# The first norm's row through DRAM instead of through TensorE

## The chip, the cores and the metric

The kernel runs on one core of one Trainium2 chip. The metric is the device time of one execution in microseconds; the median over the runs is compared. The engines are named as in the profile: PE (TensorE products) and PEld (its weight loads), DVE (VectorE), ACT (ScalarE), POOL (GpSimd), SP (SyncE, which issues nearly all transfers of this kernel).

## The reference, cut to what matters

One decoder layer on 1024 tokens of width 1024: RMSNorm, one input projection for two mixers (a gated delta rule with four heads of 128, and a dilated window attention with eight heads of 64), an output projection with residual, a second RMSNorm, a gated MLP with a short convolution, residual, and a last RMSNorm. The change touches the first norm alone:

```python
def rmsnorm(x, w):
    xf = x.astype(jnp.float32)
    y = xf * lax.rsqrt(jnp.mean(xf * xf, axis=-1, keepdims=True) + EPS)
    return (y * w.astype(jnp.float32)).astype(x.dtype)
...
    h = rmsnorm(x, norm1_w)
    proj = h @ w_in
```

The factor `rsqrt(mean(x^2) + EPS)` is one number per token. The kernel pulls it behind the projection: it multiplies x by the norm's weights only, projects, and multiplies the projection's columns by the token's factor when they leave PSUM.

## The kernel before

Activations lie transposed, with channels on the 128 partitions and the 1024 tokens along the row. Every float32 matrix is split into a high part (xhi, whi) and a rest (xlo, wlo), and a product is three products of such parts (`mm3`, L203). One product writes 512 tokens into one PSUM bank, so that a block of 128 output channels is two banks of 24 products (eight channel blocks of x by three).

The program is written as coroutines (`first`, `norms`, `gates`, `dense`, `kprep` and others), which a planner, `Weave`, runs in turn. The planner keeps a clock of PE by written estimates; a coroutine yields how long it would still wait, and the most urgent one that is ready goes on. The order that comes out is fixed for PE (`tp` and `mm` stamp an issue order on each instruction, L191 and L195). The order on the other engines and on the transfer queue is set by the framework's scheduler, which places an instruction where its inputs are ready in a simulated timeline, with the program's order as priority.

What the steps touch:

- While x is loaded, DVE adds up the squares of its eight channel blocks into `acc` (L281 on). `first` (L356) runs the first 144 products: three key blocks, into six banks `pst`, which are the two slots of each of the rings hf, asc and ch.
- `norms` (L370) sums `acc` over the partitions with eight small products, one per 128 tokens, so that the sums of the 1024 tokens lie as 128 x 8. DVE scales them (`rst`, L367), and POOL takes them to the power -1/2 (`rsqrt`, L238). Then the row has to lie on every partition, since it multiplies along the tokens: for each half, four transposes of a column of `rst`, repeated 128 times, fill a bank of the ring atr, and DVE copies it into `rstdB` (L368, 128 x 1024).
- `gates` (L396) runs beside it. It needs `rst`, not `rstdB`. At its end the running sums of the decay go to DRAM (`gdram<-grow`), and `kprep` (L577) reads them back on every partition, once for each of four heads (`dec<-gdram`).
- `scaled` (L444) multiplies a pair of banks by `rstdB`, half by half, and so empties them: `xr<-ps,rstdB` for keys, queries, values and gates, `aqkv<-ps,rstdB` for the attention. `first_keys` (L498) does it for the six banks of `first`, and goes on with the convolution of the keys on ACT and DVE (`kT`).
- `dense` (L505) waits for `first` and `norms` in the planner, loads the next weight blocks (`wst<-in_wi`), and runs the other 25 column blocks, each in two banks of the ring hf, which has two slots. A bank is overwritten only when `scaled` has emptied it.

`sy` is the wrapper around the SP queue (L139 is the wrapper's line, so all DVE, ACT, POOL and SP instructions recorded through it have that line). `rstdB` is used again, with other contents, in the second and the last norm; those are not touched.

Of the kernel before, what the change touches and what calls it, by code (L numbers as in the profile page):

```python
# [7 lines left out]
F32 = mybir.dt.float32  # L8
# [7 lines left out]
P = 128  # L16
# [128 lines left out]
def hybrid_layer(tc, I, out):  # L145
    nc = tc.nc
    wv = Weave()
    ve = Engine(wv, nc.vector, "vector", 0.07, 0.00105)
# [5 lines left out]
    sy = Engine(wv, nc.sync, "sync", 0.05, 0.00142, 2.2)  # L154
# [8 lines left out]
    dp = es.enter_context(tc.tile_pool(name="dp", bufs=1, space=DRAM))  # L163
# [15 lines left out]
    def const(name, shape, src=None):  # L179
        t = cp.tile(list(shape), F32, name=name)  # L180
        if src is not None:
            sy.dma_start(t, src)
        return t
# [6 lines left out]
    def mm(dst, lhs, rhs, us, start=True, stop=True, **kw):  # L190
        tc.stamp_issue_order_token(nc.tensor.matmul(dst, lhs, rhs, start=start, stop=stop, **kw).ins, TOKEN)  # L191
        wv.product(us, dst, lhs, rhs)

    def tp(dst, src):
        tc.stamp_issue_order_token(nc.tensor.transpose(dst, src, ident).ins, TOKEN)  # L195
        wv.product(0.11, dst, src)
# [41 lines left out]
    def rsqrt(dst, src, n):  # L238
        po_.tensor_tensor(dst, src, mhalf[:, :n], op=OP.pow)


    mixer = dp.tile([8, P, S], F32, name="mixer")
    mdram = dp.tile([H, 32, 1024], F32, name="mdram")
    gdram = dp.tile([NCH * H, P], F32, name="gdram")
# [8 lines left out]
    def bank(tag, name="ps"):  # L253
        return tile_(pp_, (P, 512), F32, name, tag, 2)

    def next_bank(tag, *tiles, slack=0.0):

        while max(wv.need(*tiles), wv.slot_free(tag, 2)) + slack > 1e-3:
            yield max(wv.need(*tiles), wv.slot_free(tag, 2)) + slack
        return bank(tag)  # L260

    def half(i):
        return slice(i * 512, i * 512 + 512)
# [103 lines left out]
    rst = const("rst", [P, NCH])  # L367
    rstdB = const("rstdB", [P, S])  # L368

    def norms():  # L370
        yield wv.need(acc, slack=8.0)
        ssp = yield from next_bank("atr", acc)
        for c in range(NCH):
            mm(ssp[:, c:c + 1], acc[:, c * P:(c + 1) * P], ones[:, :1], 0.215)
            if c % 2:
                yield APART
        ve.tensor_scalar(rst, ssp[:, :NCH], 1.0 / 1024, EPS, op0=OP.mult, op1=OP.add)
        rsqrt(rst, rst, NCH)
        wv.done.add("rst")
        yield wv.need(rst)  # L380
        for h in range(2):
            if h:
                yield wv.need(rstdB, slack=0.3)
            pb = yield from next_bank("atr")
            for c in range(4):
                i = 4 * h + c
                tp(pb[:, c * P:(c + 1) * P], rst[:, i:i + 1].to_broadcast([P, P]))
            ve.tensor_copy(rstdB[:, half(h)], pb)
        wv.done.add("norms")

    beta = sp.tile([P, NCH, H], F32, name="beta")
# [1242 lines left out]
    def mlp_down():  # L1634
# [56 lines left out]
        final_norm(0, right, ("hf", "ch"), more=squares)  # L1691

    wv.add(0, norms())
    wv.add(1, gates())
    wv.add(9, first())
# [71 lines left out]
```

## Time and profile before

| what | value |
| --- | --- |
| runs, median of 3 | 1205.56 us (1205.49 to 1207.72) |
| profiled execution, span | 1204.1 us |
| PE busy | 1194.7 us, 99% |
| DVE busy | 957.1 us, 79% |
| ACT busy | 575.9 us, 48% |
| POOL busy | 54.3 us, 5% |
| granted TensorE clock, mean | 0.998 |

The profile is of one execution, and its span runs from the first to the last instruction; the device time of a run holds some more around it. A row of a group has the source line, the engine, the operation, the tiles it writes and reads with their shapes, the count, the busy time and the mean of one. A row of the timeline has the start and the length in us, and in brackets how long the engine had been idle before and what released it. A row of the chain of waits has the start, the length and the engine whose work the end of the program hung on. A row of transfers has the queue, the count, the size of one and the median time from issue to landing. Matmuls are pipelined, so that their recorded lengths overlap; the distance from start to start is the pace.

### The profile page before, as it was taken

What the parts mean: (1) busy time and instruction counts of PE and PEld (TensorE: products, weight loads), DVE (VectorE), ACT (ScalarE), POOL (GpSimd) and SP (SyncE); (2) the same over time, 40 slices, a digit from 0 to 9 for tenths busy, and PEclk for the clock granted to TensorE, in tenths of its full rate; (3) what the DMA queues carried; (4) which work ended last, traced back from release to release, by engine and by line L of the source; (5) the groups of instructions that cost most, each with busy time, mean ns of one, the idle gap of its engine ahead of it and who ended that gap; (6) DMA issues with size and microseconds to landing.
All of it is one profiled execution on the core that took longest, in us unless ns stands there. A gap on an engine that the chain in (4) does not pass through costs nothing.

```text
span 1204.1 us, 18360 instructions
## 1 busy us (share of the span) xinstructions
PE 1194.7 (99%) x7058; PEld 987.9 (82%) x7058; DVE 957.1 (79%) x1530; ACT 575.9 (48%) x1131; POOL 54.3 (5%) x50
## 2 busy tenths in 40 slices
PE   9999999999999999999999999999999999999997
PEld 7888887898777777888888888888888888888887
DVE  7686985474667687767898989889898889898987
ACT  7383344364444444555554544444454454445452
POOL 0212110023000000000000000000000000000001
PEclk9999999999999999999999999999999999999999
DMA  7323234426433323443123132231322296357734
GB/s 236 106 75 102 77 119 122 157 79 212 166 115 106 106 63 123 150 140 140 56 85 106 59 100 89 69 105 53 105 71 86 94 370 227 109 179 223 242 97 157
DMA packets 81704, 152.72 MB, mean 127 GB/s; under 512 B 21552, under 2 KB 32592, under 8 KB 81616
## 3 DMA queue, kind: packets, MB, share of 16 engines
q1 hardware_dynamic: 80896, 151.02, 38.3%
q8 instruction: 55, 0.90, 0.3%
q10 hardware_dynamic: 720, 0.53, 0.1%
q14 instruction: 33, 0.27, 0.1%
HBM read 113.49 MB, written 35.93 MB: 124 GB/s over the span
## 4 chain that ended last, share of the span: by engine, by line
PE 98%; DVE 1%; ACT 0%; issue 0%; POOL 0%; DVEq 0%; ACTq 0%; POOLq 0%
PE ps L191 48%; PE pa L191 20%; PE dw L191 17%; PE pc L191 10%; PE ps L195 2%; PE ps L200 1%; PE warm L191 0%; DVE x1h L139 0%; ACT sm L141 0%; PE pd L191 0%; DVE sm L141 0%; POOL rs L139 0%; DVE xr L139 0%; ACT u L139 0%; ACT sq L139 0%
## 5 line engine op out<-in xcount | busy, mean ns | idle before, releaser
L191 PE MATMUL dw<-pr 128*128 128x512 f32 (+1 forms) x984 | 211.4, 377 | 0.0
L191 PEld LDWEIGHTS dw<-pr 128*128 128x128 f32 x984 | 176.8, 188 | 33.5
L191 PE MATMUL ps<-xhi,whi 128*128 128x512 f32 x448 | 186.4, 416 | 0.0
L191 PE MATMUL ps<-xhi,wlo 128*128 128x512 f32 x448 | 175.8, 392 | 0.0
L191 PE MATMUL ps<-xlo,whi 128*128 128x512 f32 x448 | 175.4, 391 | 0.0
L191 PE MATMUL pa<-T,pair 128*128 128x512 f32 x528 | 127.1, 390 | 0.1
L191 PEld LDWEIGHTS pa<-T,pair 128*128 128x128 f32 x528 | 99.0, 188 | 20.9 <-ACT u L139 0.5
L191 PEld LDWEIGHTS ps<-xhi,whi 128*128 128x128 f32 x448 | 84.7, 189 | 19.4 <-issue 2.7
L191 PEld LDWEIGHTS ps<-xhi,wlo 128*128 128x128 f32 x448 | 84.3, 188 | 18.4
L191 PEld LDWEIGHTS ps<-xlo,whi 128*128 128x128 f32 x448 | 84.9, 189 | 13.7
L139 ACT ACTIVATE u<-pa 128x512 f32<-128x512 f32 x44 | 26.3, 599 | 109.7 <-PE pa L191 109.7
L139 DVE SCALAR_TENSOR_TENSOR y<-xu,fcw,y 128x1023 f32<-128x1023 f32 (+1 forms) x44 | 56.4, 1281 | 24.4 <-ACT y L139 24.4
L139 ACT ACTIVATE pr<-wd 128x1024 fp32r<-128x1024 f32 x33 | 35.0, 1061 | 73.9 <-DVE wd L139 36.9
L139 ACT ACTIVATE whi<-wst 128x1024 fp32r<-128x1024 f32 (+2 forms) x38 | 38.6, 1015 | 62.7 <-PE ps L191 55.7
L191 PE MATMUL pa<-B,A 128*128 128x512 f32 x264 | 63.5, 390 | 0.0
L191 PE MATMUL pa<-T,S 128*128 128x512 f32 x264 | 63.4, 390 | 0.0
L191 PE MATMUL pc<-T,S 128*128 128x512 f32 x264 | 63.4, 390 | 0.0
L191 PE MATMUL pc<-B,pair 128*128 128x512 f32 x264 | 63.4, 390 | 0.0
L139 DVE TENSOR_TENSOR wst<-wst 128x512 f32<-128x512 f32 x88 | 60.5, 687 | 0.8
L191 PE MATMUL ps<-B,pair 128*128 128x512 f32 x252 | 60.6, 390 | 0.0
L141 ACT ACTIVATE sm<-sm,mx 128x128 f32<-128x128 f32 (+7 forms) x64 | 35.5, 555 | 48.1 <-DVE mx L141 48.1
L191 PEld LDWEIGHTS pa<-T,S 128*128 128x128 f32 x264 | 49.6, 188 | 10.2
(240 smaller groups left out, 2253.1 us busy)
## 6 DMA issues: line engine op xcount, KB each, us to landing
wst<-in_wu SPq DMA_DIRECT2D x44, 512.0 KB, 3.7
wd<-in_wd SPq DMA_DIRECT2D x44, 512.0 KB, 4.5
wst<-in_wi SPq DMA_DIRECT2D x25, 512.0 KB, 3.7
upark<-y SPq DMA_DIRECT2D x22, 512.0 KB, 3.7
r<-upark SPq DMA_DIRECT2D x22, 512.0 KB, 10.2
apark<-aqkv SPq DMA_DIRECT2D x12, 512.0 KB, 3.0
wa<-in_wd SPq DMA_DIRECT2D x22, 256.0 KB, 3.0
wst<-in_wo SPq DMA_DIRECT2D x8, 512.0 KB, 3.8
```

Of the source, the lines that this page charges most:

```text
L139: return getattr(eng, op)(*a, **kw)
L141: return getattr(eng, op)(*a, **kw)
L191: tc.stamp_issue_order_token(nc.tensor.matmul(dst, lhs, rhs, start=start, stop=stop, **kw).ins, TOKEN)
L195: tc.stamp_issue_order_token(nc.tensor.transpose(dst, src, ident).ins, TOKEN)
L200: tc.stamp_issue_order_token(nc.tensor.transpose(dst, src[rows], ident[rows, rows]).ins, TOKEN)
```

## The change

After `rsqrt`, the two rounds of four transposes and a copy go. In their place a new helper, `spread`, writes the 128 x 8 numbers of `rst` to a row of 1024 in DRAM in the order of the tokens, and reads this row back onto all 128 partitions of `rstdB`. Both transfers are issued on SP's queue; the second waits for the first through the DRAM tile. `norms` no longer yields after `rst`, so that the planner takes it as done at once. The row is a DRAM tile of 8 x 128 float32.

```diff
+    def spread(dst, src, name):
+
+        n_ = src.shape[-1]
+        row = dp.tile([n_, P], F32, name=name)
+        sy.dma_start(row.rearrange("c p -> p c"), src)
+        sy.dma_start(dst, bass.AP(tensor=row.tensor, offset=row.offset, ap=[[0, P], [1, n_ * P]]))
...
         wv.done.add("rst")
-        yield wv.need(rst)
-        for h in range(2):
-            if h:
-                yield wv.need(rstdB, slack=0.3)
-            pb = yield from next_bank("atr")
-            for c in range(4):
-                i = 4 * h + c
-                tp(pb[:, c * P:(c + 1) * P], rst[:, i:i + 1].to_broadcast([P, P]))
-            ve.tensor_copy(rstdB[:, half(h)], pb)
+        spread(rstdB, rst, "rrow")
         wv.done.add("norms")
```

## The prediction

> **What bounds the kernel now.** I read the page first, for the engine that is never idle, then the chain of waits around the norm, then the timelines of the engines that the row passes through.
>
> ```profile
> span 1204.1 us, 18360 instructions
> PE 1194.7 (99%) x7058; PEld 987.9 (82%) x7058; DVE 957.1 (79%) x1530; ACT 575.9 (48%) x1131; POOL 54.3 (5%) x50
> PE 98%; DVE 1%; ACT 0%; issue 0%; POOL 0%; DVEq 0%; ACTq 0%; POOLq 0%
> ```
>
> ```profile
> 5.74 31.71 PE ps L191 x166
> 37.45 0.44 PE ps L195 x4
> 37.89 2.09 PE ps L191 x9
> 39.98 0.44 PE ps L195 x4
> 40.42 20.47 PE ps L191 x91
> ```
>
> TensorE is the bound from the first products to the tail: 98% of the chain that ended last is PE, and in the norm's stretch one PE piece follows on the other with no gap. The eight transposes of the change are the two L195 pieces, 0.44 us each. They stand on the chain, so what they take is paid in full. The span is 1204.1 us and the median of the runs 1205.56 us, so some 1.5 us lie around the span; I apply the sum to the median.
>
> The row's way through the other engines:
>
> ```profile
> L139 POOL TENSOR_TENSOR rst<-rst,mhalf x1: 1639/1639/1639, 34.0 to 34.0; 128x8 f32<-128x8 f32 x1
> ```
>
> ```profile
> 38.52 0.68 DVE L139 COPY rstdB<-ps 128x512 f32<-128x512 f32 x1
> 40.45 0.69 DVE L139 COPY rstdB<-ps 128x512 f32<-128x512 f32 x1 [1.25 <-PE ps L195]
> ...
> 45.28 3.41 DVE L139 TENSOR_TENSOR xr<-ps,rstdB 128x512 f32<-128x512 f32 x5 [2.32 <-PE ps L191]
> 48.61 1.44 DVE L139 SCALAR_TENSOR_TENSOR kT<-xr,gcw,kT 128x1023 f32<-128x1023 f32 x1
> 49.97 0.68 DVE L139 TENSOR_TENSOR xr<-ps,rstdB 128x512 f32<-128x512 f32 x1
> 50.58 7.29 DVE L139 SCALAR_TENSOR_TENSOR kT<-xr,gcw,kT 128x1023 f32<-128x1023 f32 x4
> 57.79 0.68 DVE L139 TENSOR_TENSOR xr<-ps,rstdB 128x512 f32<-128x512 f32 x1
> ```
>
> rst is ready at 33.96 + 1.64 = 35.60 us, rstdB is whole at 41.14 us, and its first reader starts at 45.28 us, released not by rstdB but by PE, which has only then finished the first bank of keys. So the row is 4.1 us early, and that is the room the change has before anything waits.
>
> **What is removed.** Eight transposes: 2 x 0.44 = 0.88 us of PE on the chain. Two DVE copies of 0.68 and 0.69 us: they lie in a stretch where DVE idles anyway (1.25 us before the second, 2.32 us before the first xr), so I cost them at nothing; the price of what hid them is not asked for, since they go. The second use of the bank between the two halves goes as well.
>
> **What is added.** Two transfers on SP's queue. Who else stands there:
>
> ```profile
> 22.58 10.73 SPq L139 DMA_DIRECT2D wst<-in_wi  x4
> 41.22 0.34 SPq L139 DMA_DIRECT2D gdram<-grow  x1
> 42.78 5.66 SPq L139 DMA_DIRECT2D dec<-gdram  x4
> 65.18 0.35 SPq L139 DMA_DIRECT2D wst<-in_wi  x1
> ```
>
> From 33.3 to 41.2 us SP issues nothing. The first transfer can leave as rst appears, 35.60 us, plus a hop of 0.03 us (DVE's ba, which also waited for rst, began at 35.63 us, 0.03 after it):
>
> ```profile
> 35.63 0.23 DVE L139 TENSOR_TENSOR ba<-ps,rst 128x64 f32<-128x64 f32 x1 [1.75 <-POOL rst L139]
> ```
>
> *First transfer.* rst holds 8 words in each of 128 partitions, and neighbours in a partition land 128 words apart, so it is 1024 runs of 4 bytes, 64 for each of 16 DMA engines. No row of this trace writes 4-byte data to DRAM. The nearest:
>
> ```profile
> mdram<-um SPq DMA_DIRECT2D x16, 32.0 KB, 1.7
> x<-xdram SPq DMA_DIRECT2D x8, 64.0 KB, 2.4
> wba<-in_wba SPq DMA_DIRECT2D x1, 32.0 KB, 8.5
> gdram<-grow SPq DMA_DIRECT2D x1, 16.0 KB, 1.5
> ```
>
> ```profile
> DMA packets 1088, 0.13 MB, mean 40 GB/s; under 512 B 1088, under 2 KB 1088, under 8 KB 1088
> q1 hardware_dynamic: 1088, 0.13, 27.4%
> mdram<-um SPq DMA_DIRECT2D x4, 32.0 KB, 1.7
> ```
>
> The second fence is the stretch 83.5 to 86.8 us, in which four mdram transfers run alone. By the code each has 256 runs of 128 bytes; 4 x 256 = 1024 of the 1088 packets, so a run is a packet, and a packet costs 0.274 x 16 x 3.3 us / 1088 = 13 ns of an engine. By that rate 768 more runs cost 48 x 13 ns = 0.64 us: 2.3 us to landing. By the step from mdram (256 runs, 1.7 us) to x<-xdram (512 runs, 2.4 us), 0.7 us for each 256 runs, it is 2.4 + 1.4 = 3.8 us. Lower end: gdram's 1.5 us (32 runs). Upper end: wba, the only transfer with as many runs (1024 of 32 bytes), 8.5 us, but in the crowd of the first loads. I take 3.8 us: the dearer of the two reckonings from uncrowded rows, since 4-byte writes are unlikely to be cheaper than 128-byte ones.
>
> The Trainium skill speaks against this transfer (DMA: Bandwidth & Descriptors, Rules for kernel authors): a strided last dimension lowers to one descriptor per element, and should be rearranged until it is contiguous. The same page (Specifications) says that below 512 bytes the engine does a read-modify-write. The 128-byte packets' 13 ns show no such cost by themselves. By these packets the sum stays at 1204.7 us; if the rule bit, 4-byte words would go towards wba's end and the sum to the 1208.5 us of the second rival.
>
> *Second transfer.* 128 partitions each read the same 4 KB, 512 KB in all; it waits at the head of SP's queue until the first has landed (hop 0.06 us: gdram is issued at 41.22 and lands 1.5 us later, and dec, which reads it, is issued at 42.78). Rows of 512 KB:
>
> ```profile
> apark<-aqkv SPq DMA_DIRECT2D x12, 512.0 KB, 3.0
> wst<-in_wi SPq DMA_DIRECT2D x25, 512.0 KB, 3.7
> dec<-gdram SPq DMA_DIRECT2D x4, 512.0 KB, 7.5
> DMA to landing us min/median/max: 4.9/7.5/8.2
> ```
>
> dec is the same kind, one DRAM row read by all partitions, in 512-byte runs; four leave together, so 7.5 holds their queue and 4.9 is the one that went ahead. I take 4.9 us, with 3.0 and 8.2 as the ends.
>
> *When the row is there.* R = 35.60 + 0.03 + 3.8 + 0.06 + 4.9 = 44.4 us. Ends: 35.7 + 1.5 + 3.0 = 40.2 us, and 35.7 + 8.5 + 8.2 = 52.4 us.
>
> *When it is wanted.* PE's pace is 20.47 / 91 = 0.225 us a product. The first bank of keys is finished at about 45.2 us; 15 products of the other five banks follow, so the first dense product begins at 48.5 us, in the bank that the first xr must have emptied; the second dense unit (24 products, 5.4 us) begins at 53.9 us, and the third at 59.3 us, in the bank that the xr at 57.79 empties at 58.47 us. DVE is without a gap from 45.28 to 58.47 us, 13.2 us long. In the changed kernel PE is 0.88 us early and wants that bank at 58.4 us, so DVE must begin by 45.3 us. Up to there a late row costs nothing, and beyond it PE stalls one for one: net = -0.88 + max(0, R - 45.3). With R = 44.4 us the net is -0.88 us.
>
> *What is queued behind the wait.* Behind the second transfer stand gdram<-grow and the four dec loads; without the transposes ahead of it the gates' product can go about 1 us earlier. If the first transfer landed only at 44.2 us, they would be some 3 us late, and the first reader of dec on DVE is at 60.19 us, after the last mask on POOL (53.83 + 1.77 = 55.60 us): 4.6 us of cover.
>
> ```profile
> 53.83 1.77 POOL L139 TENSOR_SCALAR_AFFINE_SELECT dec<-dec 128x1024 f32<-128x1024 f32 x1 [0.26 <-DMA dec<-gdram]
> 60.19 0.17 DVE L139 COPY gel<-dec 128x8 f32<-128x8 f32 x1
> ```
>
> **Sum:** 1205.56 - 0.88 = 1204.7 us.
>
> **Rivals.**
>
> 1. *The saving is given back.* R falls between 45.3 and 47.1 us, and PE waits at the third dense unit for about what it saved: 1205.6 us. For it: my R is 0.9 us short of the edge. Against: mdram's packet rate puts R at 42.9.
>
> 2. *Slower: the scattered words land late.* Place: the first transfer; price: one for one beyond R = 45.3 us, slower than before from R = 46.2 us. With wba's 8.5 us and the 4.9 us of dec, R = 49.1 us, a stall of 3.8 us, 1208.5 us; with both upper ends 1205.56 - 0.88 + 7.1 = 1211.8 us. For it: only wba has as many runs. Against: wba ran among bulk loads, and SP's queue has been empty for 2.3 us.
>
> 3. *Slower: the row's second leg stands behind the dec loads.* SP works in order, and the framework's scheduler, not the hand-written order, places DMAs. If it thinks the first leg long, it puts gdram and dec ahead. The last dec landed at 53.8 us; four took 11.05 us from 42.78, 2.8 us each, so the row comes at 56.6 us: a stall of 11.3 us, 1216.0 us. Against: the row stands ahead of them in the program, and is ready 5.6 us before gdram was issued.
>
> 4. *The order of DVE and ACT shifts in the stretch that follows.* The gates are done 1 us earlier, and the key preparation hangs on them. PE's waits on other engines in the whole run are few:
>
> ```profile
> PEld ps L191 <- ACT pb L141: 2.5, 7, 0.4
> PEld ps L195 <- POOL rs L139: 1.2, 1, 1.2
> PEld ps L191 <- ACT barow L139: 0.8, 1, 0.8
> ```
>
> A good order can win little, some 2.7 us: 1202.0 us. A bad one pushes DVE operations like the 1.44 us one at 48.61 ahead of a bank's release that has 0.9 us of room (59.3 against 58.47): three of them cost some 3 us beyond the room, 1208 us.
>
> **Chances.** Forecast 0.40. Rival 1: 0.06. Rival 2: 0.22, of which 0.06 with a stall under 3.3 us (net under 2.4). Rival 3: 0.12. Rival 4: 0.20, 0.12 on the fast side and 0.08 on the slow. About 0.2% of this kernel, 2.4 us, is what its measurement can tell from no change. Within it: 0.40 + 0.06 + 0.06 = 0.52. Faster: 0.12. Slower: 0.16 + 0.12 + 0.08 = 0.36. The range goes from 1202.0 (rival 4's fast end) to 1212.0 us (both upper ends of rival 2); outside lie most of rival 3 and the far part of rival 4's fast side. The forecast alone has 1203.7 to 1206.
>
> **What would show it.** Right: PE's chain has no L195 piece between 35 and 45 us and stays without a gap to 62 us; rstdB's transfer lands before DVE's first xr, which waits for PE as before and starts near 44.4 us. The first transfer's row near 3.8 us and the second's near 4.9 us. Wrong: a first xr released by a DMA (rival 2), the second leg's issue after dec's on SP (rival 3), a PE gap near 47 or 58 us, or a difference that first opens beyond 62 us (rival 4).

## The result and the profile after

The changed kernel takes 1209.93 us (median of 8 runs, 1208.73 to 1211.07) against 1205.53 us before: a ratio of 1.0032, 95% interval 1.0023 to 1.0042. The forecast was 1204.7 us, and no difference beyond 0.2%. It is 4.4 us slower, 0.3%, by the road of the second rival.

The profiled execution took 1210.56 us. From its page, the length and the chain of waits by engine, and then the SP queue:

```profile
span 1208.8 us, 18344 instructions
...
PE 93%; issue 3%; DMA 2%; DVE 1%; ACT 1%; POOL 0%; DVEq 0%; POOLq 0%; ACTq 0%; SPq 0%
```

```profile
34.90 0.38 SPq L139 DMA_DIRECT2D rrow<-rst  x1
43.99 0.33 SPq L139 DMA_DIRECT2D rstdB<-rrow  x1
44.41 0.38 SPq L139 DMA_DIRECT2D gdram<-grow  x1
48.82 5.81 SPq L139 DMA_DIRECT2D dec<-gdram  x4
```

The first leg leaves as soon as `rst` is there and lands 9.03 us later. The second leg waits for it at the head of SP's queue and takes 4.62 us. The chain of waits runs through both; in the kernel before, no transfer had a share of the chain:

```profile
34.90 9.03 DMA rrow<-rst
...
43.99 4.62 DMA rstdB<-rrow
...
48.70 0.70 DVE xr L139
...
49.44 14.16 PE ps L191 x54
```

On DVE the first xr is now released by the transfer, after 6.04 us of idling, and on PE the first dense product waits for that xr. Timelines of the two (the row at 60.78 us is the xr that frees the bank of the third dense unit, and the product at 62.07 us is that unit's first):

```profile
48.70 3.08 DVE L139 TENSOR_TENSOR xr<-ps,rstdB 128x512 f32<-128x512 f32 x5 [6.04 <-DMA rstdB<-rrow]
...
60.78 0.68 DVE L139 TENSOR_TENSOR xr<-ps,rstdB 128x512 f32<-128x512 f32 x1
```

```profile
46.55 0.39 PE L191 MATMUL ps<-xhi,wlo 128*128 128x512 f32 x1
49.44 0.60 PE L191 MATMUL ps<-xhi,whi 128*128 128x512 f32 x1 [2.50 <-DVE xr L139]
...
50.27 0.63 PE L191 MATMUL ps<-xhi,wlo 128*128 128x512 f32 x1
...
52.83 0.52 PE L191 MATMUL ps<-xhi,wlo 128*128 128x512 f32 x1
...
62.07 0.39 PE L191 MATMUL ps<-xhi,whi 128*128 128x512 f32 x1
```

PE stands still for 2.50 us, and the products behind the gap are 0.43 us apart ((52.83 - 50.27) / 6) instead of 0.22 (20.47 us for 91 in the chain of before) for some 3.4 us. The table by stretches says why. A row has the stretch and its length, the busy time and the number of instructions of PE, PEld, DVE, ACT and POOL, and then the granted clock, the busy share of the DMA engines and GB/s:

```profile
49.70:53.10 3.40, 3.40 (x9) 2.62 (x9) 3.40 (x6) 2.30 (x2) 0.00 (x0) 0.50 0.67 160
...
575.00:579.00 4.00, 3.79 (x10) 2.97 (x11) 3.97 (x7) 2.73 (x5) 1.95 (x1) 0.57 0.00 0
```

For 3.4 us the clock is at half. Most of what this costs is hidden: the bank of the third dense unit was free at 60.78 + 0.68 = 61.46 us, and PE came to it at 62.07 us. At full clock PE would have come some 1.8 us sooner (nine products, each 0.2 us shorter) and waited there. So of these 1.8 us about 0.6 show.

There is a second stretch of low clock at the second norm, which the change does not touch. How much each place adds is read from the readers and writers of `rstdB` in the second norm, in the kernel before and then in the changed one:

```profile
L139 DVE TENSOR_TENSOR xu<-xu,rstdB x22: 1224/1226/1227, 580.7 to 980.2; 128x1024 f32<-128x1024 f32 x22
...
L139 ACT ACTIVATE rstdB<-x x2: 614/616/617, 495.0 to 496.1; 128x512 f32<-128x512 f32 x2
```

```profile
L139 DVE TENSOR_TENSOR xu<-xu,rstdB x22: 1214/1226/1226, 585.5 to 985.0; 128x1024 f32<-128x1024 f32 x22
...
L139 ACT ACTIVATE rstdB<-x x2: 614/616/617, 497.9 to 499.0; 128x512 f32<-128x512 f32 x2
```

497.9 - 495.0 = 2.9 us had been lost by the start of the second norm, 585.5 - 580.7 = 4.8 us behind it, and this holds to the last of these rows (985.0 - 980.2). So between these two profiles 2.9 us are the row's, net of what the transposes saved, and 1.9 us the second stretch's. The eight runs fall into groups by their mean clock: three at 0.998 take 1208.73 to 1209.27 us, two at 0.996 take 1209.92 and 1209.95, three at 0.995 take 1210.56 to 1211.07. A stretch of 3.4 us at half clock takes 0.0014 off the mean, so these look like runs with none, one and two such stretches; only one of the eight was profiled, with two.

Instruction by instruction, the two profiles differ only in the edit and in the gates' two small products, which moved behind six more products of the first keys; the order on the other engines is the same. Nothing else was rescheduled.

### The profile page after: what moved, and what is told of

Same layout as the page of the kernel before. It is cut to its first block, busy times and chain, and to the rows that moved or that the text cites. A ratio compares the mean times of both kernels' runs of the same rounds, so it can differ in the third digit from the quotient of the medians.

```text
span 1208.8 us, 18344 instructions
## 1 busy us (share of the span) xinstructions
PE 1196.7 (99%) x7050; PEld 987.4 (82%) x7050; DVE 955.0 (79%) x1528; ACT 575.8 (48%) x1131; POOL 55.1 (5%) x50
## 4 chain that ended last, share of the span: by engine, by line
PE 93%; issue 3%; DMA 2%; DVE 1%; ACT 1%; POOL 0%; DVEq 0%; POOLq 0%; ACTq 0%; SPq 0%
PE ps L191 44%; PE pa L191 20%; PE dw L191 17%; PE pc L191 10%; PE ps L195 2%; PE ps L200 1%; DMA rrow<-rst 1%; DMA wst<-in_wu 0%; DMA rstdB<-rrow 0%; DVE x1h L139 0%; ACT sm L141 0%; POOL rst L139 0%; DVE sm L141 0%; DVE xr L139 0%; DVE T L139 0%
```

## The experiments

**A first leg of few, long runs.** One product with the identity turns `rst` to 8 x 128.

```diff
+    rrow = const("rrow", [NCH, P])
...
-        spread(rstdB, rst, "rrow")
+        pb = yield from next_bank("atr", rst)
+        mm(pb[:NCH, :P], rst, ident, 0.11)
+        ve.tensor_copy(rrow, pb[:NCH, :P])
+        row = dp.tile([NCH, P], F32, name="rowd")
+        sy.dma_start(row, rrow)
+        sy.dma_start(rstdB, bass.AP(tensor=row.tensor, offset=row.offset, ap=[[0, P], [1, S]]))
```

> The first leg leaves as 8 runs of 512 bytes instead of 1024 of 4 bytes: one product with the identity turns rst to 8 x 128, DVE copies it to SBUF, and this goes to DRAM; the second leg is as in the changed kernel. Theory A (the 9.03 us of the first leg are the price of 1024 separate 4-byte runs): it lands in 1.5 to 2 us, as gdram<-grow did; the row is there near 42.5 us, before DVE's first xr, PE has no gap near 47 us and no clock dip after it; 8 x 0.11 us of PE go and one product comes, 1204.6 to 1205.0 us. Theory B (two dependent transfers through DRAM are too slow whatever their runs): the first leg takes over 6 us, the gap stays, 1208 us or more.

Measured: 1204.81 us against 1205.66 us before on that chip (ratio 0.9993, interval 0.9984 to 1.0002). SP's and DVE's timelines:

```profile
38.25 0.35 SPq L139 DMA_DIRECT2D rowd<-rrow  x1
39.53 0.35 SPq L139 DMA_DIRECT2D rstdB<-rowd  x1
```

```profile
44.29 3.41 DVE L139 TENSOR_TENSOR xr<-ps,rstdB 128x512 f32<-128x512 f32 x5 [0.92 <-PE ps L191]
```

The first leg is over within 1.28 us (39.53 - 38.25), the second takes 4.0 us, so that the row is there at 43.5 us. The first xr waits for PE and not for a transfer, and PE has no gap. Theory B falls: two transfers through DRAM are in time if the first is quick.

**The row as it lies, read with a stride.** The DRAM tile is P x n_, so the first leg is 128 runs of 32 bytes, and `scaled` reads `rstdB` in steps of 8 words.

```diff
-        row = dp.tile([n_, P], F32, name=name)
-        sy.dma_start(row.rearrange("c p -> p c"), src)
+        row = dp.tile([P, n_], F32, name=name)
+        sy.dma_start(row, src)
...
-                ve.tensor_tensor(t[:, sl], pair[h], rstdB[:, sl], op=OP.mult)
+                ve.tensor_tensor(t[:, sl].rearrange("p (n t) -> p n t", n=4), pair[h].rearrange("p (n t) -> p n t", n=4),
+                                        rstdB.rearrange("p (t n) -> p n t", n=8)[:, 4 * h:4 * h + 4], op=OP.mult)
```

> The first leg is written as it lies, 128 runs of 32 bytes, and the 56 readers of rstdB take it with a stride of 8 words. Theory A: 2 us for the first leg, no gap at PE, 1204.5 to 1205.0 us if the strided reads cost DVE nothing. Theory A2 (what costs is a write of a part of a line, not the number of runs): 128 such writes, an eighth of the number, 2 to 3 us, so the time is the same as by A, but the packets of 32 bytes take several times the 9 ns or so of those that are read. Theory B: over 6 us, gap as before, 1208 us. If strided reads are slower on DVE, the xr rows grow from 0.69 us and the time is above 1205.5 us by the dense stage's lack of room.

Measured: 1207.24 us (ratio 1.0014, interval 1.0005 to 1.0023). The instructions on `rst` and on `xr`:

```profile
DMA to landing us min/median/max: 1.4/1.4/1.4
```

```profile
L139 DVE TENSOR_TENSOR xr<-ps,rstdB x32: 1072/1126/1190, 44.2 to 473.4; 128x512 f32<-128x512 f32 x32
```

The first leg lands in 1.4 us, and still the kernel loses: each xr takes 1.13 us instead of 0.69, and the chain on DVE has no room for it; PE waits 0.9 us for ACT's work on the keys and 0.5 us for an xr.

**The same with the words put in order once.** The first leg is that of the kernel just shown. The second leg goes into a buffer of its own, and DVE copies it in two halves while it has nothing else to do; the readers are again those of the changed kernel.

```diff
+        mix = A("mix", "ev")
+        sy.dma_start(mix, bass.AP(tensor=row.tensor, offset=row.offset, ap=[[0, P], [1, n_ * P]]))
+        for h in range(2):
+            ve.tensor_copy(dst[:, half(h)].rearrange("p (c t) -> p c t", c=4),
+                           mix.rearrange("p (t c) -> p c t", c=NCH)[:, 4 * h:4 * h + 4])
```

> The first leg as it lies (128 runs of 32 bytes), the second into a buffer of its own, and two DVE copies put the words in order, in the stretch where DVE has nothing to do. Readers take rstdB unstrided. If the loss of the strided kernel (1207.24 us) came from its readers (xr at 1.07 us each instead of 0.69), this one is back at 1204.7 us; if it came from the 32-byte writes or from the transfers, it stays near 1207 us.

Measured: 1204.82 us against 1205.88 us before on that chip (ratio 0.9987, interval 0.9978 to 0.9996). It is 1.06 us faster than the kernel before, as much as the whole saving within the noise, and the loss of the strided kernel was its readers'.

```profile
40.22 1.24 DVE L139 COPY rstdB<-mix 128x512 f32<-128x512 f32 x2 [2.26 <-DMA mix<-rrow]
...
43.67 3.41 DVE L139 TENSOR_TENSOR xr<-ps,rstdB 128x512 f32<-128x512 f32 x5 [0.92 <-PE ps L191]
```

**The saving alone.** The kernel leaves the norm's factor out: the row is filled with ones and no transfer is made.

```diff
-        spread(rstdB, rst, "rrow")
+        ve.memset(rstdB, 1.0)
```

> The eight transposes and two copies are gone and nothing takes their place: rstdB is filled with 1.0 by one DVE instruction, so the first norm's factor is left out of the projection. It measures the saving alone. Forecast of the prediction: -0.88 us, 1204.7 us, no gap at PE. Rival (the saving is swallowed by DVE's chain of 13.2 us from the first xr on): 1205.5 us.

Measured: 1204.82 us against 1205.66 us before, 0.84 us less (ratio 0.9991, interval 0.9983 to 1.0000, which is 0 to 2 us). That fits the forecast's 0.88 us, and PE has no gap.

**What in the first leg costs.** Transfers that nothing reads, one behind the other on SP's queue, in the kernel before.

```diff
+        for name, dst, c, e in (("all", near(8, 1), 8, 1), ("eight", near(8, 8), 8, 8), ("half", near(4, 1), 4, 1),
+                                ("line", near(8, 16)[:, :, :1], 8, 1), ("row", near(8, 128)[:, :, :1], 8, 1),
+                                ("thirtytwo", near(8, 32), 8, 32), ("again", near(8, 1), 8, 1)):
+            src = sp.tile([P, c, e], F32, name=name)
+            ve.tensor_copy(src, rst[:, :c, None].to_broadcast([P, c, e]))
+            sy.dma_start(dst, src)
```

`near(n, e)` is a DRAM region of n x 128 x e words, laid out so that partition p's share of column c stands at (c, p).

> The kernel before, with seven transfers more on SP's queue after the norm, each waiting for the one ahead; nothing reads them, and their landings are what counts, not the time of the kernel, which grows by their sum. 'all' is the first leg of the change (1024 words of 4 bytes into 4 KB), 'half' has 512 of them, 'line' has 1024 words 64 bytes apart, 'row' 1024 words 512 bytes apart, 'eight' 1024 runs of 32 bytes, 'thirtytwo' 1024 runs of 128 bytes, 'again' repeats 'all' (the last two stand beside dec's loads). Theory A (each short run costs a share of its own): all 9, half 5.2, line 9, row 9, eight 9, thirtytwo 4 us. Theory A2 (words that share a piece of memory are written one after the other): all 9, half 5, but line and row 2 to 4 us, since there each word has its own; eight 2 to 4 us. Theory E (a fixed latency of 7 us or more after any such transfer, whatever the number): half 8 us or more.

Transfers of this kernel, each made once, the last column being the time to landing:

```profile
far<-thirtytwo SPq DMA_DIRECT2D x1, 128.0 KB, 6.8
...
far<-eight SPq DMA_DIRECT2D x1, 32.0 KB, 2.5
far<-all SPq DMA_DIRECT2D x1, 4.0 KB, 9.6
far<-half SPq DMA_DIRECT2D x1, 2.0 KB, 9.0
far<-line SPq DMA_DIRECT2D x1, 4.0 KB, 4.1
...
far<-row SPq DMA_DIRECT2D x1, 4.0 KB, 2.9
far<-again SPq DMA_DIRECT2D x1, 4.0 KB, 12.9
```

As many runs of 32 bytes land in 2.5 us, and as many words 512 bytes apart in 2.9, so theory A falls. Half the words still take 9.0 us; that would speak for theory E, but "row" has the same kind of write and lands soon. What "all" and "half" share is how densely the words lie. "again", the same transfer as "all" with dec's loads beside it, took 12.9 us; "thirtytwo", also beside them, 6.8 where theory A expected 4. "line" (words 64 bytes apart) took 4.1 us, longer than "row".

**Words farther apart.** The same with every word, every second, fourth and eighth.

```diff
+        for name, dst, c, e in (("every", near(8, 1), 8, 1), ("second", near(8, 2)[:, :, :1], 8, 1), ("fourth", near(8, 4)[:, :, :1], 8, 1),
+                                ("eighth", near(8, 8)[:, :, :1], 8, 1)):
```

> The kernel before with four transfers more on SP's queue, each waiting for the one ahead and read by nothing; their landings count. Each has 1024 words of 4 bytes: every word of 4 KB ('every', the change's first leg), every second word of 8 KB, every fourth of 16 KB, every eighth of 32 KB. Theory A2 (words that fall into the same 64 bytes of DRAM are written one after the other; 16, 8, 4 and 2 of them do): 9.6, some 5.8, 4.2 and 3.4 us, on a line to the 2.9 us of words 512 bytes apart. Theory G (only whether neighbours touch, in one stretch of 4 KB, matters): 9.6 us, and 3 us for the other three.

```profile
far<-every SPq DMA_DIRECT2D x1, 4.0 KB, 9.9
far<-second SPq DMA_DIRECT2D x1, 4.0 KB, 4.5
far<-fourth SPq DMA_DIRECT2D x1, 4.0 KB, 3.3
far<-eighth SPq DMA_DIRECT2D x1, 4.0 KB, 2.7
```

**Fewer words, longer runs.**

```diff
+        for name, dst, c, e in (("one", near(1, 1), 1, 1), ("two", near(8, 2), 8, 2), ("four", near(8, 4), 8, 4), ("eight", near(8, 8), 8, 8)):
```

> The same with 128 words of 4 bytes into 512 bytes ('one'), then 1024 runs of 8, 16 and 32 bytes, dense. Theory A2: the time goes with the writes in the same 64 bytes (16, 8, 4, 2), not with the number of runs: 'one' 8 us or more although it has an eighth of the runs, then about 5.8, 4.2 and 2.5 us. Theory A: 'one' 2.2 us, the others 9 us, as the number of runs goes.

```profile
far<-eight SPq DMA_DIRECT2D x1, 32.0 KB, 2.2
far<-one SPq DMA_DIRECT2D x1, 0.5 KB, 8.0
far<-two SPq DMA_DIRECT2D x1, 8.0 KB, 4.8
far<-four SPq DMA_DIRECT2D x1, 16.0 KB, 3.5
```

128 words of 4 bytes in 512 bytes take 8.0 us, more than 1024 runs of 32 bytes. The two series agree: with 16 writes in each 64 bytes the landing is 8.0 to 9.9 us, with 8 it is 4.5 to 4.8, with 4 it is 3.3 to 3.5, with 2 it is 2.2 to 2.7, whether the writes are words with holes between them or dense runs. The number of writes matters far less: at 16 in 64 bytes 128 of them take 8.0 us and 1024 take 9.0 to 9.9; at 2 in 64 bytes, 128 take 1.4 us (the strided kernel's first leg, over the same 4 KB as the change's) and 1024 take 2.2 to 2.7. Theory G falls: every second word took 4.5 us against its 3, and the dense runs of 32 bytes, which touch each other, 2.2.

Theory A2 holds in its order from 16 to 2, not in its sizes: 8 writes were to take 5.8 us and took 4.5 to 4.8. With one write in 64 bytes it no longer orders anything ("row" 2.9 us, "line" 4.1). The store of `grow`, issued 0.41 us behind "line", does not explain that one: the same store followed "eighth" as closely, and it landed in 2.7 us. How large the shared piece is, 32 bytes or 64 or more, the runs do not tell, nor whether it matters that different DMA engines write into the same piece.

**Late for another reason.** The first experiment's kernel with transfers of 4 KB from DRAM to DRAM ahead of the second leg, three in one kernel, two in the other.

```diff
+        for i in range(3):
+            hop = dp.tile([NCH, P], F32, name=f"hop{i}")
+            sy.dma_start(hop, row)
+            row = hop
```

> The first experiment's kernel (8 runs of 512 bytes), with three more transfers of 4 KB from DRAM to DRAM ahead of the second leg, some 1.8 us each: no scattered word, but a row that comes at about 49 us. Theory F (what costs is only when the row lands, one for one beyond 45.3 us): -0.8 + 3.7 = +2.9 us, 1208.5 us, PE stands still near 47 us, and the clock is low behind it in some runs. Rival (the scattered writes themselves hold up other traffic): the row is as late, but the kernel stays within 1 us of the 1204.8 us of the first experiment.

> As the kernel with three hops, with two of them, so that the second leg stands ahead of dec's loads on SP's queue: the row comes at about 48.6 us, as in the changed kernel, without a scattered word. Theory F (only the landing counts): -0.8 + 3.3 = +2.5 us and up to 2 us more where the clock is low at the second norm, 1208.4 to 1210.4 us, PE's gap 2 to 3.3 us, the changed kernel's own time. Rival (scattered writes cost beyond their lateness): 1207 us or less at the same landing.

With three, 1217.37 us (ratio 1.0084, interval 1.0070 to 1.0098), far more than expected, since the scheduler put two of dec's loads ahead of the second leg, and it took 8.4 us beside them:

```profile
45.18 1.16 SPq L139 DMA_DIRECT2D dec<-gdram  x2
46.70 1.56 SPq L139 DMA_DIRECT2D rstdB<-hop  x1
```

```profile
rstdB<-hop SPq DMA_DIRECT2D x1, 512.0 KB, 8.4
```

This is the third rival's place, though not in the changed kernel. With two, 1208.78 us (1207.74 to 1210.91) against 1205.64 us before on that chip (ratio 1.0026, interval 1.0016 to 1.0035). DVE's timeline and PE's waits:

```profile
47.86 3.68 DVE L139 TENSOR_TENSOR xr<-ps,rstdB 128x512 f32<-128x512 f32 x6 [4.78 <-DMA rstdB<-hop]
```

```profile
PE ps L191 <- DVE xr L139: 2.3, 2, 1.2
```

The row comes 0.8 us earlier than in the changed kernel's profile, and the kernel loses 3.1 us instead of 4.4. A row that is late without a scattered word costs nearly what the changed kernel loses, so the scattered writes cost by their lateness; what is left for them beyond it is under 1 us. The loss looks different in the profile: the clock stays full, and PE waits twice, 1.2 us for the first bank and 1.1 us for the third unit's. The copy is not exact either, since some instructions of DVE and ACT run in another order here.

**PE kept at work through the gap.**

```diff
         wv.add(2, first_keys())
+        for _ in range(2):
+            pb = yield from next_bank("atr")
+            for _ in range(5):
+                mm(pb[:, :P], warm, warm, 0.225)
```

> The changed kernel with ten more products of 128 columns (2.25 us by the rows of the first products of this kind, 20 in 4.5 us) after the last product of the first three key blocks, into a bank that is free; nothing reads them. Theory C (the low clock after the gap, 9 products at 0.43 us instead of 0.226, comes from PE's standing still): PE stands still for less than 0.7 us, the clock stays at 1.00 behind it, and the kernel gains the 1.7 us of the dip wherever it had one: about 1208.2 us, against 1209.9 us. Theory D (the dip belongs to the dense stage's start or to the transfers that land there): the dip stays, and the time is 1209.9 us or some more.

Measured: 1211.69 us (1211.23 to 1212.09), against 1209.93 us of the changed kernel. Stretches and waits of PE:

```profile
49.00:51.00 2.00, 0.79 (x6) 0.56 (x5) 1.15 (x2) 0.00 (x0) 0.00 (x0) 1.00 0.05 19
51.00:53.00 2.00, 2.00 (x10) 1.62 (x9) 2.00 (x5) 1.79 (x2) 0.00 (x0) 1.00 0.53 152
```

```profile
PE ps L191 <- DVE xr L139: 2.1, 2, 1.2
PE ps L195 <- ACT sq L141: 1.4, 1, 1.4
```

The low clock is gone, as theory C has it, but the time is 1.8 us longer and not 1.7 us shorter, as it was expected to be. PE, now at full pace, reaches the third dense unit before DVE has emptied its bank (the second wait for xr). Besides, the first leg took 9.6 us here, so that the first xr began 1.15 us later than in the changed kernel's profile (49.85 against 48.70 us); and DVE and ACT run in another order behind it, probably because the planner counted the ten products, and a wait of 1.4 us for ACT is new. The test is not clean. It fits the reading that a low clock behind the gap is mostly covered by DVE's chain.

**The changed kernel again.**

> The changed kernel unaltered, beside the others on the same chip: 1209.9 us. A second profile shows what is firm in it and what chance: the first leg's 9.0 us and PE's gap of 2.5 us should come again within half a us; of the two stretches with a low clock (behind the gap and at the second norm), each may be missing.

Measured: 1210.17 us (1209.77 to 1212.39; ratio 1.0031, interval 1.0021 to 1.0042).

```profile
rrow<-rst SPq DMA_DIRECT2D x1, 4.0 KB, 9.9
```

```profile
PE ps L191 <- DVE xr L139: 3.3, 1, 3.3
```

The first leg took 9.9 us, PE's gap was 3.3 us, both more than half a us beyond the first profile's; low clocks stood at both places. So the landing itself moves by about 1 us.

## Why the prediction was wrong

**What bounds the kernel, and the saving:** right, as far as the interval tells. Without the row the kernel gains 0.84 us, and 0.88 was forecast.

**The first transfer:** here the prediction failed. "I take 3.8 us" was 9.0 to 9.9 us, above even the upper end of 8.5. The working counted runs, at 0.7 us for 256 more, and both of its rows move runs of 128 bytes; one of them, x, is a load from DRAM and no store. The packets were indeed soon done. The DMA's busy share in the stretch 34.9 to 44.0 us of the changed kernel, in 40 slices, and its packets:

```profile
DMA  5410695000000000000000000000000000200000
...
DMA packets 1085, 0.14 MB, mean 15 GB/s; under 512 B 1056, under 2 KB 1056, under 8 KB 1083
```

The 1056 short packets are the 1024 words, one each, and a few more. All but 22 of them are over after seven slices of 0.23 us, 1.6 us; the last 22 run 2.6 to 2.7 us after the issue (the busy slice at 42.6 us is another queue's single packet), and the landing comes 6.3 us behind them. So the count of runs said little: the time goes with how many writes fall into the same small piece of DRAM. What happens there in those 6.3 us no trace shows. The Trainium skill's read-modify-write below 512 bytes (DMA: Bandwidth & Descriptors, Specifications) fits only in part: runs of 32 bytes, far below 512, land in 1.4 to 2.5 us.

**The second transfer:** 4.62 us against 4.9 us, right.

**R and the net:** the form was right, the input not. With the row landed at R, the prediction's net is -0.88 + max(0, R - 45.3) (-0.8 where one product stays). The column with PE's own place is explained below the table:

| kernel | R, us | by the formula, us | with PE's own place, us | measured median, us | lowest, us |
| --- | --- | --- | --- | --- | --- |
| turned | 43.5 | 1204.8 | 1204.8 | 1204.81 | 1204.38 |
| two hops | 47.8 | 1207.3 | 1207.8 | 1208.78 | 1207.74 |
| changed | 48.6 | 1208.0 | 1208.8 | 1209.93 | 1208.73 |
| changed, again | 50.1 | 1209.5 | 1209.6 | 1210.17 | 1209.77 |
| three hops | 55.1 | 1214.6 | 1214.4 | 1217.37 | 1216.27 |

For the four late rows the lowest runs lie 0.3 to 1.7 us above the formula, the medians up to 2.8. The formula lacked two things.

The first is that its 45.3 us holds for one execution. What counts is how late the row is for PE, and PE's place differs from profile to profile. The last product of the first keys, in the kernel before and in the changed one:

```profile
48.25 0.39 PE L191 MATMUL ps<-xhi,wlo 128*128 128x512 f32 x1
```

```profile
46.55 0.39 PE L191 MATMUL ps<-xhi,wlo 128*128 128x512 f32 x1
```

Of these 1.70 us the transposes are 0.88; by the other 0.82 us PE was simply further on, and so it wanted the row at 44.5 us and not at 45.3. In the other profiles that product begins at 46.97 us (two hops), 47.23 (changed, again) and 47.62 (three hops). The column with PE's own place corrects for it. The lowest runs of the late rows lie within 0.2 us of that column, but for the three hops; they are other executions than the profiled ones, so part of this closeness may be luck.

The second is the low clock. At the second norm it also comes with a row that is in time: the first experiment's slowest run, 1206.92 us, was profiled and has a clock of 0.70 between 570 and 575 us, and no gap on PE near 47 us. There its price is in full, 1.9 us; behind the gap most of it is hidden. In the three hops' profile PE's gap is 7.9 us and the clock is at half until 61.2 us, which is the likely reason for the rest there.

**The rivals:** the second came true at its own place and by the sign that was named for it, a first xr released by a transfer, with R = 48.6 against its 49.1 us. Its 1208.5 us lacked the same two things. I gave it 0.22, because wba's 8.5 us looked like crowding; it was the better guide, but by luck: wba is a load in runs of 32 bytes, and 1024 runs of 32 bytes to DRAM landed in 2.2 to 2.5 us. The third did not happen in the changed kernel (SP's order is the second leg, then gdram, then dec). The fourth did not either: no order changed but for the edit and the gates' two products.

**What is queued behind:** right for gdram, which left at 44.41 us, 3.2 us later than before. dec left 6.0 us later (48.82 against 42.78 us), since gdram took 4.4 us to land beside the second leg instead of 1.5. Nothing waited for it, but the cover of 4.6 us had shrunk to 1.4: the last mask on POOL ended at 61.81 us, and its first reader on DVE began at 63.19.

## What to carry to other kernels

Price a transfer by its landing, not by its packets: a store that spreads single words densely over DRAM had nearly all its packets done in 1.6 us and landed after 9. Turn the data first, or write it as it lies in runs of 32 bytes or more and put it in order on an engine that has time; then the detour through DRAM did pay here, by about 1 us. A row whose readers stand on a gapless chain is wanted by the length of that chain before the bound engine's next need; work that point out from the bound engine's own progress and compare landings with it.

## What the runs showed that was not expected

Writes of 4 bytes, densely side by side, land in 8.0 to 9.9 us whether they are 128, 512 or 1024; every second word alone takes 4.5 us, and words 512 bytes apart 2.9.

A gap of 2.5 us on PE was followed by 3.4 us at half clock, gaps of 1.21 us (the filled kernel) and 1.25 us (two hops) by none; at the second norm the low clock came without a gap of note, behind sixteen products of one column, in some executions and not in others. The Trainium skill (TensorE: Matmul & The Clock Gate, Part 1) describes a gate that looks at activity in free-running windows of about 3.4 us. The traces agree with this more closely than the tables show. In their records of the clock, each low stretch inside the 13 profiled runs lasts 3.41 us or three times that, and the clock changes only at whole multiples of 3.413 us from its first change: in the changed kernel it is full for 44.37, 522.24 and 624.64 us, 13, 153 and 183 times that length. Where these cuts fall differs from run to run, since the first change comes 4.1 to 7.3 us after the first instruction.

With 0.227 us for a product of 512 columns, one can add up how far products fill each piece between two cuts. In the 13 profiles every piece at full clock that was filled to less than 0.38 was followed by half clock and none that was filled to more than 0.40 was; between the two this estimate cannot part them. The piece with the sixteen thin products is filled to 0.39 in the changed kernel, where the clock fell, and to 0.46 in the kernel before, where it did not. So it seems to depend on where the cuts fall whether a thin stretch costs anything; no run here moved the cuts alone.
